# Pairs' weights reach the expert table by indirect word transfers in place of one-hot products

## The chip, the cores and the metric

The kernel runs on one core of one Trainium2 chip. Its time is the device time of one execution in microseconds (us), and lower is better. All times of one core here agree closely: three runs of the kernel before lie between 1845.62 and 1847.0 us. TensorE is called PE in the profile, VectorE DVE, ScalarE ACT, GpSimd POOL (Pool) and SyncE SP.

## What is computed

One decoder block for 512 tokens of 1024 values: an HGRN2 mixer and a dilated-window attention in parallel, then a PEER layer that picks experts. The change lies in the PEER layer alone. For each token and each of 8 heads, 16 of 128 x 128 experts are picked by two lists of 128 keys; expert number = i1 * 128 + i2.

```python
def peer_ffn(x, w_q, sub_keys, u, v):
    q = (x @ w_q).reshape(B, S, PEER_HEADS, 2, PEER_HALF)
    s = jnp.einsum('bshpc,hpnc->bshpn', q, sub_keys).astype(jnp.float32)
    s1, i1 = lax.top_k(s[..., 0, :], PEER_TOPK)
    s2, i2 = lax.top_k(s[..., 1, :], PEER_TOPK)
    ...
    top_s, pos = lax.top_k(cand_s, PEER_TOPK)
    idx = jnp.take_along_axis(cand_i, pos, axis=-1)
    gate = jax.nn.softmax(top_s, axis=-1)
    ...
        hid = jnp.einsum('thkd,td->thk', u[ib], xb)
        a = jax.nn.gelu(hid.astype(jnp.float32), approximate=False) * gb
        return jnp.einsum('thk,thkd->td', a.astype(x.dtype), v[ib])
```

A pair is one token with one picked expert: 512 x 8 x 16 = 65536 pairs. Two heads of one token may pick the same expert, and then their weights add up.

## The kernel before

**Tiles.** The 512 tokens are four tiles of 128, T = 0 to 3. Tiles 1 and 2 (`UD`) take the hidden values u.x of all 16384 experts by streaming the whole of u through PE. Tiles 0 and 3 (`UG`) gather the 128 rows of u that each token's pairs name. Tiles 1, 2 and 0 (`VD`) take the product with v by streaming the whole of v; tile 3 gathers its rows of v. A gather is one indirect transfer from Pool's queue of 128 rows of 4 KB, one for each token, and an instruction of DVE uses it (`u_steps`, L626; `v_steps`, L645; the transfer is issued at L618).

**The table.** The streamed product with v works by blocks b of 128 experts (all i1 for one i2). For that it needs a table of weights [i1, i2, token] that is zero except at the pairs. Before, `scatter_steps` makes it for 16 tokens at a time: DVE compares the pairs' key numbers with a ramp (one-hot rows `e12`, L666), multiplies those of i2 by the weights in three bfloat16 parts (`eg`, L670; for some groups ACT makes the third part, L674), PE multiplies the two for each token (three products a token, L680), ACT copies the result into `Gx` (L682), and SP writes it to DRAM (`g_d`, L685). The first eight blocks of tiles 0 and 2 stay on chip in `Gcs[0]` by a copy of Pool (L687). `thirds` makes the three parts, and `routing` ends with transposes of the key numbers and gates for it.

**Stages.** (1) `Front(0)`: the mixers of the first 256 tokens, with weights loaded by SP and split into two parts; the profile ends it near 300 us. (2) `Front(1)`: the mixers of the second half. Between its loads `background` puts steps of two queues of work: `rows` (gathers of tile 0) and `scat` (the table of tile 1). `routing(0)` and `routing(1)` lie here too; the latter's key numbers are ready at 566 us. (3) The stage between: `routing(2)`, the table of tiles 1, 0 and 2, `NPRE` = 46 calls of `hidden(b)`, and `routing(3)`. `hidden` loads a 512 KB block of u (`ub`), splits it (`uh` on ACT, `ul` on Pool for the first 46, on DVE after), makes 24 matmuls (`ph`) and a Gelu into `pre`, of which there are `RING` = 58 places. (4) The main loop of 128 blocks: the table of eight blocks comes in one load `Gc` (L822); DVE multiplies it by `pre` (L825); it and a 512 KB block of v (`vb`) are split in two; 18 matmuls `acc` follow (L834); then `hidden(b + NPRE)`, and two gather steps of tile 3.

**Order.** The instructions of each engine run in the order that a planner sets when the program is built: it follows the program's order where operands are expected to be ready, and takes later work where they aren't. What waits at the head of an engine's queue holds all behind it. A place of the ring `pre` lets up to 58 hidden blocks stand ahead of the main loop.

Of the kernel before, what the change touches and what calls it, by code (L numbers as in the profile page):

```python
# [8 lines left out]
F32 = mybir.dt.float32  # L9
# [9 lines left out]
P = 128  # L19
S = 512  # L20
D = 1024
# [16 lines left out]
# Token tiles by how the expert layer reaches them: rows of u gathered, u streamed whole, v streamed whole.  # L38
# VD starts with UD; the tile that is not in it gathers its rows of v.
# [5 lines left out]
GT = 16  # L45
NGT = NV // GT
GB = 8
# the first weights' low halves are Pool's
LPOOL = 4
# steps of gathering and scattering before the end of the second half's mixers  # L50
ROWS_P, SCAT_PP = 99, 5
# blocks of hidden values ahead of the products with v, and places for them
NPRE, RING = 46, 58
# tokens in a group of the scatter, groups in flight; groups whose third part ACT scales
GS, EGB = 4, 2
ACT3 = {1: (0, 4, 8, 12), 0: (0, 4, 8, 12), 2: (0, 8)}
ROWS_F, ROWS_D, SCAT_F = 3, 2.0, 0.4
UK, WBUFS, ATB = 4, 4, 3

# columns of the packed per-partition parameters  # L60
C_G1, C_HGN, C_LB, C_QG, C_KG, C_END = 0, 8, 9, 17, 18, 19
# columns of the packed shape constants
M_ATT, M_HG, M_END = 0, 512, 640
# slots of the packed dense weights
# [4 lines left out]
def kernel(ctx: ExitStack, tc: tile.TileContext, x, wst, par, cst, cols, g2, keys, u, v, ut, vr, out):  # L69
# [9 lines left out]
    nc.scalar.activation(root, eps[:, 0:1], AF.Sqrt)  # L79
    h2g = {}  # L80
# [17 lines left out]
    def accumulate(out, ws, xs, cut, w_stays):  # L98
        """Sum over the blocks of w x, in three products where they come in two parts."""
# [24 lines left out]
    # lower bound: softmax over the two logit rows, row 0  # L124
# [5 lines left out]
    # values of the first group by token; of the other two with every fourth token's in a row  # L130
# [13 lines left out]
    class Front:  # L144
        """The mixers of one half of the tokens, and the queries of their expert layer."""

        def __init__(self, h, hi_pool, after_unit):
# [5 lines left out]
            for t in range(NT):  # L153
# [5 lines left out]
                for c in range(0, KC, 4):  # L159
# [20 lines left out]
        def slot(self, i, ks=slice(0, KC)):  # L180
            """Row blocks ks of a slot's weights, UK of them in a tile: the blocks' operands in order."""
# [14 lines left out]
        def proj(self, i, x, T):  # L196
            """A slot's 256 columns of the half's products with x, on the partitions (T) or along them."""
# [112 lines left out]
        def proj_attn(self):  # L310
# [47 lines left out]
            # with the scores' scale of 1 / 8  # L358
# [69 lines left out]
        def proj_gates(self):  # L428
# [6 lines left out]
            # behind the last exponential: the functions' tables take turns  # L435
# [5 lines left out]
        def post(self):  # L441
            """Merge, output projection, second norm and expert queries."""
# [22 lines left out]
            for b in range(4):  # L465
# [13 lines left out]
            for t in range(NT):  # L479
# [21 lines left out]
                # x1 waits in the output rows it belongs to  # L501
# [21 lines left out]
    def thirds(i, x):  # L523
        """x as the exact sum of three bfloat16."""
        w, dst = pk3[:, i], pk[:, i, 2:]
        nc.vector.tensor_copy(dst[:, 0], x)
        nc.vector.tensor_tensor(out=w, in0=x, in1=dst[:, 0], op=ALU.subtract)
        nc.vector.tensor_copy(dst[:, 1], w)
# [374 lines left out]
```

## Time and profile before

| | |
|---|---|
| median of three runs | 1846.65 us (1845.62 to 1847.0) |
| profiled execution: span | 1845.0 us |
| PE busy | 1674.0 us |
| DVE busy | 1444.1 us |
| ACT busy | 795.6 us |
| Pool busy | 793.6 us |
| moved by DMA | 475.61 MB, 258 GB/s over the span |

The profiled execution's own time is its span, 1845.0 us; the median is 1.65 us longer. Busy time is an average over stages, so the stages are read one by one. A PE that is busy isn't PE at its peak: the granted clock (1.00 is 2.4 GHz, 0.50 is 1.2 GHz) has to be read beside it. Pool counts an indirect transfer as busy for the time in which it writes out the transfer's descriptors, not for the time in which the data move.

### The profile page before, as it was taken

Reading aid. Unit: us, or ns where it says so; the run is one execution under the profiler, and the core shown is the slowest. Engines: PE = TensorE matmul, PEld = TensorE weight load, DVE = VectorE, ACT = ScalarE, POOL = GpSimd, SP = SyncE. Lnnn points to the kernel's source line nnn. Section 1 sums busy time; section 2 is a strip of 40 time slices with the busy share of each in tenths; the row PEclk is TensorE's granted clock in tenths of the full one; section 3 lists DMA queues with packets and bytes.
Section 4 is the critical chain, followed back from the end, with each engine's and each line's share of the span. In section 5 each row is a group of like instructions: output and inputs, shape, how many; then the busy total and the mean of one; then the engine's idle time right before and its main releaser. Section 6 shows DMA issues by size and latency. Waiting matters only on the chain.

```text
span 1845.0 us, 28370 instructions
## 1 busy us (share of the span) xinstructions
PE 1674.0 (91%) x10573; PEld 1482.8 (80%) x10573; DVE 1444.1 (78%) x2681; ACT 795.6 (43%) x1348; POOL 793.6 (43%) x546
## 2 busy tenths in 40 slices
PE   6999889889789989888867899999999999999987
PEld 6998888667667878777867878888888888888766
DVE  5644547887887758999999977877877788888777
ACT  5655551211114556368756534343343434343232
POOL 3211312463664335556566543344323464444442
PEclk9999999988899989889978899999999999999999
DMA  6453553778787887534455799999988999999887
GB/s 196 153 158 119 175 194 118 270 235 276 244 279 264 297 298 261 183 111 145 152 183 202 238 372 334 339 328 326 367 298 299 345 339 341 340 340 317 288 309 278
DMA packets 169963, 475.61 MB, mean 258 GB/s; under 512 B 14304, under 2 KB 62688, under 8 KB 168800
## 3 DMA queue, kind: packets, MB, share of 16 engines
q1 hardware_dynamic: 112416, 270.56, 43.0%
q0 software_dynamic: 55296, 201.35, 30.9%
q10 hardware_dynamic: 2112, 1.88, 0.3%
q8 instruction: 83, 1.36, 0.3%
q14 instruction: 56, 0.46, 0.1%
HBM read 443.85 MB, written 28.84 MB: 256 GB/s over the span
## 4 chain that ended last, share of the span: by engine, by line
PE 47%; DVE 25%; DMA 11%; issue 9%; POOL 5%; ACT 1%; DVEq 0%; POOLq 0%; SPq 0%; ACTq 0%
PE acc L834 19%; PE pp L109 13%; PE ph L109 10%; DMA row<-in_u_dram,idx 6%; DVE row L626 4%; DVE e L666 4%; DVE eg L670 3%; POOL row L618 3%; DMA Gc<-g_d 3%; PE pg L680 2%; PE pr L680 1%; DVE cs L564 1%; DVE rest L515 1%; DVE ti L514 1%; DVE h2g L645 1%
## 5 line engine op out<-in xcount | busy, mean ns | idle before, releaser
L618 POOL DMA_INDIRECT row<-in_u_dram,idx x206 | 254.9, 1237 | 383.8 <-DVE row L626 274.3
L626 DVE SCALAR_TENSOR_TENSOR row<-row,h2g 128x1024 f32<-128x1024 f32 x206 | 272.4, 1328 | 62.2 <-DMA row<-in_u_dram,idx 61.3
L109 PE MATMUL ph<-hH,uh 128*128 128x256 f32 x1024 | 302.1, 295 | 7.1 <-ACT pre L792 6.0
L109 PE MATMUL ph<-hH,ul 128*128 128x256 f32 x1024 | 302.9, 296 | 5.0 <-POOL ul L95 5.0
L109 PE MATMUL ph<-hL,uh 128*128 128x256 f32 x1024 | 299.0, 292 | 0.0
L834 PE MATMUL acc<-vl,ah 128*128 128x512 f32 x768 | 241.8, 396 | 9.3 <-DVE vl L95 9.3
L834 PE MATMUL acc<-vh,al 128*128 128x512 f32 x768 | 240.0, 393 | 0.0
L94 ACT ACTIVATE uh<-ub 128x1024 fp32r<-128x1024 f32 x128 | 136.7, 1068 | 230.7 <-PE ph L109 214.1
L834 PE MATMUL acc<-vh,ah 128*128 128x512 f32 x768 | 222.5, 395 | 9.9 <-ACT vh L94 9.9
L109 PEld LDWEIGHTS ph<-hH,uh 128*128 128x128 f32 x1024 | 205.9, 201 | 12.8 <-ACT pre L792 7.8
L109 PEld LDWEIGHTS ph<-hH,ul 128*128 128x128 f32 x1024 | 205.5, 201 | 6.3 <-POOL ul L95 5.8
L109 PEld LDWEIGHTS ph<-hL,uh 128*128 128x128 f32 x1024 | 204.6, 200 | 3.8
L680 PEld LDWEIGHTS <-e 128*128 128x128 bf16 x1152 | 124.8, 119 | 73.4 <-DVE eg L670 65.4
L834 PEld LDWEIGHTS acc<-vl,ah 128*128 128x128 f32 x768 | 143.2, 190 | 40.0 <-DVE vl L95 11.8
L834 PEld LDWEIGHTS acc<-vh,ah 128*128 128x128 f32 x768 | 142.9, 190 | 38.2 <-ACT vh L94 10.5
L834 PEld LDWEIGHTS acc<-vh,al 128*128 128x128 f32 x768 | 145.5, 190 | 31.8
L94 ACT ACTIVATE ah<-Gc 128x384 fp32r<-128x384 f32 x128 | 66.9, 523 | 229.4 <-PE acc L834 226.7
L95 DVE TENSOR_TENSOR vl<-vb,vh 128x1024 fp32r<-128x1024 f32 x128 | 156.1, 1219 | 12.2 <-ACT vh L94 12.0
L618 POOL DMA_INDIRECT row<-in_v_dram,idx x76 | 111.6, 1469 | 120.0 <-DVE h2g L645 109.2
L680 PE MATMUL pg<-eg,e 128*128 128x128 bf16 x768 | 103.1, 297 | 51.8 <-DVE eg L670 51.3
L94 ACT ACTIVATE vh<-vb 128x1024 fp32r<-128x1024 f32 x128 | 135.6, 1059 | 28.6 <-DMA vb<-in_vr_dram 27.9
L674 ACT ACTIVATE eg<-e,pk 128x128 bf16<-128x128 bf16 x320 | 115.4, 565 | 70.9 <-DVE e L666 68.1
(279 smaller groups left out, 3582.4 us busy)
## 6 DMA issues: line engine op xcount, KB each, us to landing
w<-in_wst_dram SPq DMA_DIRECT2D x140, 512.0 KB
ub<-in_ut_dram SPq DMA_DIRECT2D x128, 512.0 KB
vb<-in_vr_dram SPq DMA_DIRECT2D x128, 512.0 KB
Gc<-g_d SPq DMA_DIRECT2D x15, 1536.0 KB
g_d<-Gx SPq DMA_DIRECT2D x16, 960.0 KB
g_d<-Gx SPq DMA_DIRECT2D x8, 1024.0 KB
row<-in_u_dram,idx POOLq DMA_INDIRECT x206
sc<-in_x_dram SPq DMA_DIRECT2D x4, 512.0 KB
```

The source lines that it names most:

```text
L94: nc.scalar.activation(hi, x, AF.Copy)
L95: (eng or nc.vector).tensor_tensor(out=lo, in0=x, in1=hi.bitcast(F32), op=ALU.subtract)
L109: nc.tensor.matmul(out, l, r, start=(i == 0), stop=(i == len(ops) - 1))
L514: nc.vector.max_index(out=ids[:, 0:8], in_max=vals[:, 0:8], in_values=src)
L515: nc.vector.match_replace(out=rest[:, :w], in_to_replace=vals[:, 0:8], in_values=src, imm_value=-BIG)
L618: nc.gpsimd.indirect_dma_start(out=r, out_offset=None, in_=src, in_offset=bass.IndirectOffsetOnAxis(ap=index, axis=0))
L626: nc.vector.scalar_tensor_tensor(r, r, 1.0, h2g[T], op0=ALU.mult, op1=ALU.mult, accum_out=hid[:, g, j:j + 1])
L666: nc.vector.tensor_tensor(out=e12, in0=iota[:, None].to_broadcast([P, 2, NKEY, GS]), in1=e[:, 0:2].to_broadcast([P, 2, NKEY, GS]), op=ALU. ...
L670: last_e2[0] = nc.vector.tensor_tensor(out=eg[:, :n], in0=e12[:, 1:2].to_broadcast([P, n, NKEY, GS]), in1=e[:, 2:2 + n].to_broadcast([P, n ...
L674: nc.scalar.activation(eg[:, 2, :, q], e12[:, 1, :, q], AF.Copy, scale=pk3[:, VD.index(T), i + k + q:i + k + q + 1])
L680: nc.tensor.matmul(pt[:, q], e12[:, 0, :, q0 + q], eg[:, j, :, q0 + q], start=(j == 0), stop=(j == 2))
L834: nc.tensor.matmul(acc[t][c], lt, r[:, c * 512:(c + 1) * 512], start=(b == 0 and i == 0), stop=(b == NKEY - 1 and i == 2))
```

## The change

The table [i1, i2, token] of each tile in `VD` lies in DRAM by itself. It is cleared during `Front(0)` by twelve transfers of 2 MB from ACT's queue, one behind every fourth load of weights. `routing` only makes, for each pair, its place in the table (128 x expert number + token) in one instruction of DVE. `spread_steps` then issues, for each of a tile's 128 pairs of a token (8 heads x 16), one indirect transfer of 128 words, one a token, that adds the word to the table. The 16 transfers of a head wait for all 16 of the head before, so that no two additions to one word are under way at once; the loads of `Gc` wait for the last head of each tile. For tiles 1 and 2 the words are the gates, and for tile 0 they are the gates times the Gelu of the gathered hidden values.

One-hot rows, their products, ACT's copies, `thirds` and the transposes in `routing` are gone. `Gc` is loaded in three transfers of 512 KB, in runs of 4 KB, where it was one of 1536 KB in runs of 512 B. `ul` of all hidden blocks is DVE's. `NPRE` goes from 46 to 60 and `RING` from 58 to 72. `routing(3)` and the gathers of tile 3 come between the hidden blocks, from b = 16 on, half a gather for each block; in the main loop it is 1.9 for each. Removed comments are left out below.

```diff
-GT = 16
-NGT = NV // GT
+ROWS_P, SCAT_PP = 99, 110
+NPRE, RING = 60, 72
+ROWS_F, ROWS_H, ROWS_D, SCAT_F = 3, 0.5, 1.9, 3
+RT3 = 16
...
+    tok = const.tile([P, 1], F32, name="tok")
+    nc.scalar.dma_start(out=tok, in_=par[:, C_TOK:C_TOK + 1])
...
         if T in VD:
-            pt = route_bank(T)
-            i12 = rt.tile([P, 2, P], F32, name="i12")
...
-            if T in UD:
-                nc.tensor.transpose(pt[:, 3], gate, ident)
-                thirds(VD.index(T), pt[:, 3])
+            nc.vector.tensor_scalar(place[:, VD.index(T)], full, float(P), tok, op0=ALU.mult, op1=ALU.add)
...
-    def scatter_steps(T, bank):
...
+    def spread_steps(T):
+        i = VD.index(T)
+        w = gates[:, T] if T in UD else hid[:, UG.index(T)]
+        for j in range(P):
+            d = nc.gpsimd.indirect_dma_start(out=g_d[i].rearrange("i j t -> (i j t)")[:, None], in_=w[:, j:j + 1],
+                                             out_offset=bass.IndirectOffsetOnAxis(ap=place[:, i, j:j + 1], axis=0),
+                                             in_offset=None, compute_op=ALU.add)
...
+            if j % TOPK == 0:
+                before, spread[i] = spread[i], []
+            behind(d, before)
+            spread[i].append(d)
             yield 1
...
+        zero = whi.tile([P, D], F32, name="zero", bufs=1)
+        nc.gpsimd.memset(zero, 0.0)
+        clear = [(g, k) for g in g_d for k in range(0, NKEY, 32)]
+        def clearing(load):
+            if f_units[0] % 4 == 3 and clear:
+                g, k = clear.pop(0)
+                with tc.issue_after(load.ins):
+                    nc.scalar.dma_start(out=g[:, k:k + 32].rearrange("p (a b) t -> p a (b t)", b=8),
+                                        in_=zero[:, None].to_broadcast([P, 4, D]))
...
-    scat.add(scatter_steps(1, pr_bank))
+    scat.add(spread_steps(1))
...
+    scat.add(spread_steps(0))
...
-        ubs = halves(us.tile([P, KC, P], F32R, name="uh"), us.tile([P, KC, P], F32R, name="ul"), ub,
-                     nc.gpsimd if b < NPRE else nc.vector)
+        ubs = halves(us.tile([P, KC, P], F32R, name="uh"), us.tile([P, KC, P], F32R, name="ul"), ub)
...
         routing(2, rq2)
-        scat.add(scatter_steps(0, pg_bank))
-        scat.add(scatter_steps(2, pg_bank))
-        scat(P)
+        scat.add(spread_steps(2))
+        scat(2 * P)
         for b in range(NPRE):
+            if b == RT3:
+                routing(3, rq3)
+                h2g[3] = const.tile([P, D], F32, name="h2g")
+                nc.sync.dma_start(out=h2g[3], in_=h2_d)
+                rows.add(u_steps(3))
             hidden(b, php)
-        routing(3, rq3)
...
+            rows(ROWS_H)
...
         if b % GB == 0:
-            Gc = Gcs[0]
-            if b:
-                Gc = (vs if b // GB % 2 else dp).tile([P, NGT, GB, GT], F32, name="Gc", bufs=1)
-                nc.sync.dma_start(out=Gc, in_=g_d[:, :, b:b + GB])
+            Gc = (vs if b // GB % 2 else dp).tile([P, len(VD), GB, P], F32, name="Gc", bufs=1)
+            for t, g in enumerate(g_d):
+                behind(nc.sync.dma_start(out=Gc[:, t], in_=g[:, b:b + GB]), spread[t])
```

## Rows read from the trace of the kernel before

**Rows 1.** Stages; columns: length, busy us (instructions) by engine, granted clock, DMA share, GB/s.

```profile
565.00:1066.00 501.00, 417.81 (x2912) 384.80 (x2910) 439.92 (x907) 303.88 (x589) 268.76 (x174) 0.90 0.63 214
1066.00:1845.00 779.00, 752.51 (x4128) 653.57 (x4128) 622.68 (x795) 289.92 (x407) 320.33 (x228) 0.98 0.92 327
```

**Rows 2.** Chain that ended last, main loop; columns: start us, length us, what.

```profile
1126.00 2.84 PE ph L109 x24
1128.84 4.14 PE acc L834 x18
...
1453.94 17.67 DMA Gc<-g_d
...
1710.00 16.46 DMA Gc<-g_d
...
1754.29 19.05 DMA Gc<-g_d
...
1778.99 54.50 PE acc L834 x237
```

**Rows 3.** Groups by line, the scatter's; columns: busy us, mean ns, idle before, releasers.

```profile
L674 ACT ACTIVATE eg<-e,pk 128x128 bf16<-128x128 bf16 x320 | 115.4, 565 | 70.9 <-DVE e L666 68.1 <-DVE pk L529 2.7
L666 DVE TENSOR_TENSOR e<-iota,pk 128x1024 bf16<-128x1024 bf16 x96 | 103.8, 1089 | 27.5 <-PE pr L680 20.7 <-PE pg L680 6.6
L680 PE MATMUL pg<-eg,e 128*128 128x128 bf16 x768 | 103.1, 297 | 51.8 <-DVE eg L670 51.3 <-issue 0.3
L670 DVE TENSOR_TENSOR eg<-e,pk 128x1024 bf16<-128x1024 bf16 x96 | 103.0, 1082 | 0.1
...
L680 PE MATMUL pr<-eg,e 128*128 128x128 bf16 x384 | 50.0, 297 | 6.4 <-DVE eg L670 4.2 <-ACT eg L674 2.0
```

**Rows 4.** Instructions on tile e: duration ns min/median/max, first and last start us.

```profile
L666 DVE TENSOR_TENSOR e<-iota,pk x96: 660/686/3107, 567.5 to 1044.1; 128x1024 bf16<-128x1024 bf16 x96
```

**Rows 5.** Pool in order of time; columns: start us, length us, instruction, idle before it.

```profile
918.30 1.35 POOL L618 DMA_INDIRECT row<-in_u_dram,idx  x1 [0.30 <-issue]
919.96 0.94 POOL L618 DMA_INDIRECT row<-in_u_dram,idx  x1 [0.30 <-issue]
921.20 1.05 POOL L618 DMA_INDIRECT rq<-in_u_dram,idx  x1 [0.30 <-issue]
922.55 0.94 POOL L618 DMA_INDIRECT rq<-in_u_dram,idx  x1 [0.30 <-issue]
923.51 2.35 POOL L95 TENSOR_TENSOR ul<-ub,uh 128x1024 fp32r<-128x1024 f32 x1
```

**Rows 6.** Stages, gathers (line 618) alone; columns: length, Pool busy us (count), clock, DMA.

```profile
0.00:565.00 565.00, 95.28 (x81) 0.94 0.62 202
565.00:1066.00 501.00, 88.66 (x76) 0.90 0.63 214
```

**Rows 7.** Groups by line: Pool's part of routing, and the split of u on DVE.

```profile
L95 DVE TENSOR_TENSOR ul<-ub,uh 128x1024 fp32r<-128x1024 f32 x82 | 101.1, 1233 | 53.7 <-ACT uh L94 51.6 <-ACT ah L94 1.2 <-issue 0.7
...
L582 POOL TENSOR_TENSOR sel<-eq,ci 128x800 f32<-128x800 bf16 x32 | 54.5, 1704 | 56.1 <-DVE eq L580 55.9
...
L584 POOL TENSOR_TENSOR sel<-sel 128x400 f32<-128x400 f32 x32 | 40.8, 1276 | 0.7
```

**Rows 8.** Chain that ended last, second half's mixers: gathers from issue to use.

```profile
316.67 10.17 DMA row<-in_u_dram,idx
...
555.09 5.29 DMA row<-in_u_dram,idx
```

**Rows 9.** Stages, tile ph alone; columns: length, busy PE, PEld, ACT, clock, DMA.

```profile
565.00:1066.00 501.00, 192.20 (x1248) 177.94 (x1248) 18.94 (x51) 0.90 0.63 214
```

**Rows 10.** DMA queues of the page: packets, MB, share of 16 engines' span.

```profile
q0 software_dynamic: 55296, 201.35, 30.9%
q10 hardware_dynamic: 2112, 1.88, 0.3%
```

More of the change, by code (lines that the diff above doesn't have):

```diff
@@ L44 @@
 NV = len(VD) * P
-GT = 16
-NGT = NV // GT
 GB = 8
+GS = 4
 LPOOL = 4
[L51 to L57, printed above, removed]
+ROWS_P, SCAT_PP = 99, 110
+NPRE, RING = 60, 72
+ROWS_F, ROWS_H, ROWS_D, SCAT_F = 3, 0.5, 1.9, 3
+RT3 = 16
 UK, WBUFS, ATB = 4, 4, 3
-C_G1, C_HGN, C_LB, C_QG, C_KG, C_END = 0, 8, 9, 17, 18, 19
+C_G1, C_HGN, C_LB, C_QG, C_KG, C_TOK, C_END = 0, 8, 9, 17, 18, 19, 20
 M_ATT, M_HG, M_END = 0, 512, 640
@@ L521, in route_bank @@
         return pt.rearrange("p (n k) -> p n k", k=NKEY)
[L523 to L528, printed above, removed]
-        nc.vector.tensor_tensor(out=w, in0=w, in1=dst[:, 1], op=ALU.subtract)
-        nc.vector.tensor_copy(dst[:, 2], w)
     def routing(T, rq):
         gate = gates[:, T]
-        full = rt.tile([P, P], F32, name="full")
+        full = fulls[:, VD.index(T)] if T in VD else rt.tile([P, P], F32, name="full")
         sv = rt.tile([P, PH, TOPK], F32, name="sv")
@@ new lines, with behind @@
+    spread = {i: [] for i in range(len(VD))}
+    def behind(d, others):
+        for o in others:
+            tc.add_manual_dep(d.ins, o.ins.name, mybir.DependencyInfo(mybir.DependencyClass.Sync, mybir.DependencyReason.DATA),
+                              reason="pairs of one expert")
+    def spread_steps(T):
[5 more added lines that the diff above has]
+                                             in_offset=None, compute_op=ALU.add)
+            tc.declare_no_dep(d.ins, group=f"spread{i}{j // TOPK}", reason="heads are ordered below")
+            tc.add_to_no_dep_group(f"spread{i}{j // TOPK}", d.ins)
+            if j % TOPK == 0:
+                before, spread[i] = spread[i], []
+            behind(d, before)
+            spread[i].append(d)
@@ L711 @@
     rows, scat = Pump(), Pump()
+    dram = ctx.enter_context(tc.tile_pool(name="dram", bufs=1, space=bass.MemoryType.DRAM))
+    h2_d = dram.tile([P, D], F32, name="h2_d")
+    g_d = [dram.tile([P, NKEY, P], F32, name=f"g_d{i}") for i in range(len(VD))]
     rq_pool = ctx.enter_context(tc.tile_pool(name="rq", bufs=2, side="left"))
@@ L742 @@
     hid = gat.tile([P, len(UG), P], F32, name="hid", bufs=1)
-    pk = gat.tile([P, len(VD), 5, P], BF16, name="pk", bufs=1)
-    pk3 = gat.tile([P, len(VD), P], F32, name="pk3", bufs=1)
     rctx = ctx.enter_context(ExitStack())
-    gb = rctx.enter_context(tc.tile_pool(name="gb", bufs=1, side="left", **TILE))
     rt = rctx.enter_context(tc.tile_pool(name="rt", bufs=1, side="left", **TILE))
+    fulls = rt.tile([P, len(VD), P], F32, name="fulls", bufs=1)
+    place = rt.tile([P, len(VD), P], I32, name="place", bufs=1)
     pr = rctx.enter_context(tc.tile_pool(name="pr", bufs=2, space=PSUM, side="left"))
@@ L760 @@
     routing(1, rq1)
-    pr_bank = lambda: pr.tile([P, 512], F32, name="pr")
-    scat.add(scatter_steps(1, pr_bank))
+    scat.add(spread_steps(1))
     f.hgrn(0)
@@ L778 @@
     pre = []
-    Gcs = [dp.tile([P, NGT, GB, GT], F32, name="Gc")]
-    nc.sync.dma_start(out=Gcs[0][:, :P // GT], in_=g_d[:, :P // GT, :GB])
     def hidden(b, pool):
@@ L792, in hidden @@
         nc.scalar.activation(dst, pt, AF.Gelu)
-    with tc.tile_pool(name="php", bufs=2, space=PSUM, side="right") as php, \
-            tc.tile_pool(name="pg", bufs=3, space=PSUM, side="right") as pg:
-        pg_bank = lambda: pg.tile([P, 512], F32, name="pg")
+    with tc.tile_pool(name="php", bufs=4, space=PSUM, side="right") as php:
         routing(2, rq2)
-        scat.add(scatter_steps(0, pg_bank))
-        scat.add(scatter_steps(2, pg_bank))
-        scat(P)
+        scat.add(spread_steps(2))
+        scat(2 * P)
         for b in range(NPRE):
-            hidden(b, php)
-        routing(3, rq3)
-    h2g[3] = const.tile([P, D], F32, name="h2g")
-    nc.sync.dma_start(out=h2g[3], in_=h2_d)
-    rows.add(u_steps(3))
-    with tc.issue_after(last_e2[0].ins):
-        rows(4)
+            if b == RT3:
[3 more added lines that the diff above has]
+                rows.add(u_steps(3))
+            hidden(b, php)
+            rows(ROWS_H)
     rows.add(v_steps(3))
@@ L831 @@
             for i, (l, r) in enumerate([(aH, vH), (aH, vL), (aL, vH)]):
-                lt = l.rearrange("p g t -> p (g t)")[:, t * P:(t + 1) * P]
+                lt = l[:, t]
                 for c in range(2):
```

55 lines of the change are left out of this document (7 added, 48 removed).

## The prediction, made before the changed kernel was seen

> **What bounds the kernel now.** I read the stages first, then the chain of work that ended last, then the groups by line for what the change touches, and last the order of time on Pool, because the change moves its work there.
>
> The stages split at two points. Up to 565 us the mixers run, and the change hardly touches them. From 565 to 1066 us the table is made. Here DVE is busy for 440 of 501 us, Pool for 269, and PE for 418 at a clock of 0.90; from 1066 on PE is busy for 753 of 779 us at 0.98 [rows 1]. So the stage between is DVE's, and the main loop is PE's.
>
> What ends the stage between is the table: the one-hot instructions of DVE run from 567.5 to 1044.1 us [rows 4], and the products with v can't start before all three tiles are in it. The main loop adds up from the chain: a hidden block costs PE 2.84 us and a block of v 4.14 [rows 2]. 1248 of the `ph` matmuls, 52 blocks of 24, lie before 1066 [rows 9], so PE still owes 76 x 2.84 + 128 x 4.14 = 216 + 530 = 746 us. From the end of the last matmuls (1778.99 + 54.50 = 1833.5 [rows 2]) to the span's end there are 11.5 us. 1066 + 746 + 11.5 = 1823.5; the 21 us that are missing to 1845 fit the three late loads of `Gc`, which stand in the chain with 16 to 19 us each, partly behind earlier PE work [rows 2].
>
> So the end is M + what PE owes at M, where M is the start of the products with v. Both terms change.
>
> **What goes.** DVE loses 103.8 + 103.0 us of one-hot work, ACT 115.4 and its copies of the products, PE 1152 matmuls with 153 us of busy time [rows 3]. On DVE and PE this is time of the stage between, and none of it is in the main loop [rows 4]. DVE gets `ul` of the first blocks from Pool: 60 x 1.233 = 74 us [rows 7]. DVE then needs 440 - 207 - 7 (the three-part split and the transposed numbers, an estimate from its few short instructions) + 74 = 300 us in that stage; at its former share of 440 / 501 it would be through at 565 + 300 / 0.88 = 906. If nothing else bound it, M would be there. The gain on DVE is real, but it isn't the end of the sum.
>
> **What comes.** Pool gets 384 indirect transfers of words. The trace shows none of them; the nearest row is the gather of 128 rows, which also has 128 places, one for each token. Where Pool has nothing to wait for, a gather takes 0.94 us and the next starts 0.30 us later: 919.96 to 921.20 is 1.24 us [rows 5]. Bounds of the cadence: below, 0.94 with hardly any gap (Pool's next instruction of another kind follows in 0.02 us [rows 5]), 0.96; above, the stage's mean of 88.66 / 76 = 1.17 [rows 6] and the gap, 1.47. A word is less than a row for the DMA engines, but Pool writes the descriptor of a place, not its bytes; the addition may need more of it, and the missing wait for a buffer less. I take 1.24, the row nearest in kind and undisturbed.
>
> The words of tile 1 can start when `routing(1)` is through, at 565 as before. From there to M Pool must do: the 128 - 81 = 47 gathers of tile 0 that are left [rows 6] and 384 words, 431 x 1.24 = 534 us; its part of `routing(2)` and `routing(3)`, half of 54.5 + 40.8, 48 us [rows 7]; four additions of the mixers, about 7 us; and of the up to 22 gathers of tile 3 that stand between the hidden blocks, half, 14 us. Together 603.
>
> **The heads.** A tile's next head waits at the head of Pool's queue, and behind it stand the other tiles' words, the gathers and the routing steps that DVE waits for. A gather takes 5.3 to 10.2 us from issue to use [rows 8], with 512 KB in it. With 8 heads a tile, 7 of them waiting, 21 such waits are 111 to 214 us if nothing lies between, and nothing if two tiles take turns. Tile 1 is alone with the gathers at first, tiles 0 and 2 can alternate: I take four bare waits of 5.3, 21 us.
>
> By the Trainium skill, "DMA: Bandwidth & Descriptors", section "Anatomy of one DMA — SWDGE (gpsimd) path", a transfer that Pool issues has a fixed cost of about 2.0 us, most of it the receipt of the last write, and the heaviest target is DRAM. By that the 21 waits would be 42 us at most, and the four 8. No row here shows a bare transfer of words, so it stays at the gather's 5.3.
>
> **Smaller parts.** The clearing is 24 MB during the first mixers, whose stage up to 565 has a DMA share of 0.62 at 202 GB/s [rows 6]. It is hidden under PE while the loads of weights keep their lead; without that cover it costs 24 MB at the main loop's 327 GB/s [rows 1], 73 us. I take 4. PE's relief at the end of the second mixers is worth nothing while Pool is behind. After the last head there is its landing (5), the first `Gc` (8, as three small gathers) and its product and split (7, from the first step after the stall at 1453.94 to the matmuls): 20 us.
>
> M = 565 + 4 + 603 + 21 + 20 = 1213, where it was 1066.
>
> **What PE owes at M.** Before, 52 blocks were done between `NPRE` 46 and `RING` 58; I take the middle of 60 and 72 again, 66. 62 x 2.84 + 530 = 706. The loads of `Gc` in runs of 4 KB should be late less often: 10 us of the 21. With the 11.5 at the end: 728.
>
> 1213 + 728 = 1941, against the profiled span of 1845.0; the median lies 1.65 above that span. **Forecast: 1940 us, slower by 5%.** The one-hot work leaves DVE and PE, which were full, but the table gets done on Pool, which was half idle, and in a queue of one after another that needs longer than DVE did.
>
> **Rivals.**
>
> *A word is cheap on Pool (faster).* Place: Pool's queue from 565 to M. If the 0.30 us before a gather belongs to its wait for a buffer, or a word's descriptor to less work, the cadence falls. At 0.96 the sum loses 384 x 0.28 = 107 us: 1833. At half a gather, 0.62, it loses 238: 1702. It decides against my sign from 1.24 - 97 / 384 = 0.99 us on. For it: Pool follows a transfer by another instruction in 0.02 us. Against it: four gathers in a row all show 0.30 [rows 5]. I give it 1780 and 0.27.
>
> *The words bind the DMA engines (much slower).* Place: the same stage, on 16 engines. 384 word transfers have as many packets as the 384 gathers that make up q0, 55296. A gather's packet takes 0.309 x 16 x 1845 us / 55296 = 165 ns, a packet of q10 with 890 bytes 0.003 x 16 x 1845 / 2112 = 42 ns [rows 10]. The stage used 0.63 x 501 = 316 us of every engine [rows 1]. With 3456 packets an engine, the words fit into the 648 us up to M while one takes under 96 ns. An addition in DRAM reads and writes; at 165 ns it needs 570 us, M becomes 565 + 316 + 570 + 20 = 1471, and the end 2199. Waits for heads lengthen in the same case, since a head's last word lands behind its queue. I give it 2150 and 0.15.
>
> The Trainium skill, "DMA: Bandwidth & Descriptors", section "Specifications", speaks for this one: under 512 B a DMA engine reads, modifies and writes. By that rule every word is two passes over memory. No row here has such a packet.
>
> *It comes out even.* Where the cadence is near 0.99 the two sides meet: 0.04, 1846.
>
> **How the numbers follow.** The forecast, slower by 1% to 8%, has 0.54; the cheap word 0.27; the full DMA engines 0.15; even 0.04. Some 0.2% is what a measurement of this kernel can tell from no change. Faster is 0.27, same 0.04, slower 0.69. The forecast's own range takes the cadence from 1.05 to 1.47 and the heads from none to half of 214: 1860 to 2070. The range for 8 in 10 takes in part of the first rival, down to a cadence of about 0.9 (1800), and part of the second, up to some 125 ns a word packet (565 + 316 + 432 + 20 + 728 = 2061, and a little for the heads): 1800 to 2080.
>
> **What would show it.** Right: Pool nearly without a gap from 565 to the first `acc` matmul, words 1.2 to 1.3 us apart, the chain through Pool's queue there, PE idle with its ring of 72 full, first `acc` near 1210, and then 6.98 us for each block with a hidden block in it. The first rival: words under 1 us apart, first `acc` before 1110, and the chain on DVE or PE. The second: Pool waiting at every 16th word, or short instructions with long gaps; a DMA share near 1 with few GB/s. The forecast is wrong above all if words cost Pool less than rows do, and it errs on the high side if the planner puts words ahead of what else Pool has to do.

## The result, and the profile after

After the change the kernel takes 2245.12 us (median of four, 2238.74 to 2248.49), before it 1846.83 in the same runs: a ratio of 1.2147, 95% interval 1.2115 to 1.218. It is slower by 21%. The direction and the place of the loss are those of the forecast, the size isn't: 305 us over 1940, outside the range. The profiled execution took 2246.77 us, 1.87 more than its span of 2244.9.

The first 300 us of the kernel after, and its two later stages, cut where its words start (585) and at the first product with v (1554); columns as in [rows 1]: length, busy us (instructions) of PE, PEld, DVE, ACT and Pool, granted clock, DMA share, GB/s.

```profile
0.00:300.00 300.00, 234.72 (x1999) 221.97 (x2000) 120.78 (x196) 133.10 (x213) 61.14 (x32) 0.97 0.61 219
...
585.00:1554.00 969.00, 388.84 (x2520) 354.81 (x2520) 336.91 (x823) 143.29 (x234) 802.83 (x514) 0.70 0.50 114
1554.00:2245.00 691.00, 672.54 (x3504) 576.80 (x3504) 583.38 (x751) 256.29 (x354) 298.19 (x220) 0.99 0.92 342
```

The stage between takes 969 us where it took 501 [rows 1], and in it Pool is the only engine that is busy for most of the time. DVE, which had 440 of 501 us, has 337 of 969, and PE 389. The main loop is shorter: 691 us, not 779.

The words on Pool, by tile of the table: duration in ns (min/median/max), first and last start.

```profile
L643 POOL DMA_INDIRECT g_d<-gates,place x256: 1547/1552/2692, 584.9 to 1517.1; - x128
L643 POOL DMA_INDIRECT g_d<-hid,place x128: 1551/1556/2654, 1075.6 to 1471.7; - x128
```

Three of them in order of time (start, length, what, idle time before it):

```profile
1300.00 1.55 POOL L643 DMA_INDIRECT g_d<-hid,place  x1 [0.30 <-issue]
1301.85 1.55 POOL L643 DMA_INDIRECT g_d<-hid,place  x1 [0.30 <-issue]
1303.71 1.55 POOL L643 DMA_INDIRECT g_d<-hid,place  x1 [0.30 <-issue]
```

Line 643 alone, from 585 to 1519: length, Pool busy us (count), clock, DMA share, GB/s.

```profile
585.00:1519.00 934.00, 639.76 (x384) 0.70 0.49 107
```

An adding word transfer takes Pool 1.55 us, and the next starts 0.30 us later: 1.855 us where nothing disturbs, against 1.24 of a gather [rows 5]. Over the stage it is more: 639.76 us busy for 384, and 115.4 us of idle time before them (76.6 + 38.8, below), 1.97 us a word.

The groups by line, of PE's wait and of the words: busy us, mean ns, idle time before, and what ended most of it.

```profile
L110 PE MATMUL ph<-hH,uh 128*128 128x256 f32 x1024 | 304.0, 297 | 370.0 <-ACT pre L770 338.7
L643 POOL DMA_INDIRECT g_d<-gates,place x256 | 425.3, 1661 | 78.7 <-issue 76.6
L643 POOL DMA_INDIRECT g_d<-hid,place x128 | 214.5, 1676 | 38.8 <-issue 38.8
```

A stretch late in the words, in the columns of the first fence:

```profile
1200.00:1520.00 320.00, 7.91 (x61) 7.30 (x60) 29.32 (x51) 3.71 (x5) 269.27 (x177) 0.52 0.30 33
```

PE waits 338.7 us for `pre`, 314 of them in one wait that ends at 1524.8: the ring of 72 places is full, and no product with v can take a block out. From 1200 to 1520 us hardly any engine but Pool works. The DMA engines are 0.30 busy there and move 33 GB/s, so they aren't the bound. "issue" as the releaser means that the profile shows nothing for which a word waited.

The Trainium skill describes this picture in "Perfetto Trace Analysis", section "What 'DMA-bound' means": a kernel can be bound by the queue that issues transfers, whose track is then solid with slices that are the writing of descriptors, not the moving of data. The rows agree as far as they go: the words hold Pool for 755 of the 934 us from 585 to 1519, gaps included, at a DMA share of 0.49.

The chain of waits at the end of the stage (start, length, what):

```profile
1517.08 1.55 POOL g_d L643
1518.63 1.07 POOL sel L576
...
1522.98 5.84 DMA row<-in_u_dram,idx
...
1541.49 1.14 DVE ul L96
1542.84 0.15 SPq L766
1543.09 0.38 SPq L800
...
1545.42 17.44 DMA Gc<-g_d
```

SP's issues there, in order of time:

```profile
1520.18 0.33 SPq L795 DMA_DIRECT2D Gc<-g_d  x1
1536.50 6.49 SPq L766 DMA_DIRECT2D ub<-in_ut_dram  x2
1543.09 1.54 SPq L800 DMA_DIRECT2D vb<-in_vr_dram  x3
```

The last word ends at 1518.6, the first product starts at 1553.8. In these 35 us SP issues `Gc`, which waited for the last word at the head of its queue, then two blocks of u, and only then the first blocks of v. Most of the time goes to the blocks of u: 22.6 us lie between the issues of `Gc` (1520.5) and of v (1543.1), and for 21.8 of them SP waits for DVE ahead of the two blocks: 15.9 us end with a `ul`, 5.9 just behind the next `ul`. This instruction is the last to read a block of u, and here it stands on DVE among the gather steps of tile 3.

The start is late too. ACT from 13 to 53 us, in order of time (start, length, what, idle before it):

```profile
13.89 15.93 ACTq L693 DMA_DIRECT2D g_d<-zero  x3
29.86 1.06 ACT L95 ACTIVATE wh<-w 128x1024 fp32r<-128x1024 f32 x1 [15.70 <-issue]
29.88 5.30 ACTq L693 DMA_DIRECT2D g_d<-zero  x1
35.23 0.63 ACT L95 ACTIVATE hH<-pT 128x512 fp32r<-128x512 f32 x1 [4.31 <-issue]
35.25 16.72 ACTq L693 DMA_DIRECT2D g_d<-zero  x3
52.02 0.63 ACT L95 ACTIVATE hH<-pT 128x512 fp32r<-128x512 f32 x1 [16.17 <-issue]
```

All twelve clearing transfers are issued between 4.4 and 52.1 us, not one behind every fourth load: the order was set against loads on SP's queue, and ACT's queue didn't wait for these (SP had issued at most eight loads of weights by then). While ACT issues them, it does nothing else for 4 to 16 us at a time. PE gets its first `hH` late and is busy for 235 of the first 300 us. In the kernel before it was 273:

```profile
0.00:300.00 300.00, 273.48 (x2331) 258.55 (x2332) 158.97 (x287) 153.41 (x252) 63.89 (x32) 0.98 0.50 157
```

### The profile page after: what moved, and what is told of

It is laid out like the page before. It is cut to its first block, busy times and chain, and to the rows that moved or that the text cites. A ratio compares the mean times of both kernels' runs of the same rounds, so it can differ in the third digit from the quotient of the medians.

```text
span 2244.9 us, 25786 instructions
## 1 busy us (share of the span) xinstructions
PE 1543.9 (69%) x9412; PEld 1363.0 (61%) x9412; DVE 1274.6 (57%) x2511; ACT 597.4 (27%) x932; POOL 1292.4 (58%) x869
## 3 DMA queue, kind: packets, MB, share of 16 engines
q0 software_dynamic: 110592, 201.57, 32.4%
## 4 chain that ended last, share of the span: by engine, by line
PE 25%; POOL 20%; issue 6%; DMA 3%; DVE 1%; ACT 0%; SPq 0%; DVEq 0%; POOLq 0%; ACTq 0%
PE acc L806 18%; POOL g_d L643 17%; PE ph L110 6%; POOL row L599 1%; DMA vb<-in_vr_dram 1%; POOL rq L599 1%; DMA Gc<-g_d 1%; DMA rq<-in_v_dram,idx 0%; DMA g_d<-gates,place 0%; DMA row<-in_u_dram,idx 0%; POOL sel L576 0%; DVE row L607 0%; DVE idf L577 0%; ACT vh L95 0%; DVE h2g L622 0%
## 5 line engine op out<-in xcount | busy, mean ns | idle before, releaser
L110 PE MATMUL ph<-hH,uh 128*128 128x256 f32 x1024 | 304.0, 297 | 370.0 <-ACT pre L770 338.7
L643 POOL DMA_INDIRECT g_d<-gates,place x256 | 425.3, 1661 | 78.7 <-issue 76.6
L607 DVE SCALAR_TENSOR_TENSOR row<-row,h2g 128x1024 f32<-128x1024 f32 x206 | 277.3, 1349 | 223.9 <-DMA row<-in_u_dram,idx 223.3
L599 POOL DMA_INDIRECT row<-in_u_dram,idx x206 | 249.2, 1210 | 252.0 <-DVE row L607 147.6
L643 POOL DMA_INDIRECT g_d<-hid,place x128 | 214.5, 1676 | 38.8 <-issue 38.8
L806 PE MATMUL acc<-vh,ah 128*128 128x512 f32 x768 | 208.8, 392 | 10.0 <-ACT vh L95 10.0
L96 DVE TENSOR_TENSOR ul<-ub,uh 128x1024 fp32r<-128x1024 f32 x128 | 160.3, 1253 | 89.5 <-ACT uh L95 87.9
L577 DVE TENSOR_REDUCE idf<-sel 128x16 f32<-128x400 f32 x32 | 26.3, 823 | 314.6 <-POOL sel L576 314.6
L96 POOL TENSOR_TENSOR wl<-w,wh 128x1024 fp32r<-128x1024 f32 (+1 forms) x22 | 55.2, 2511 | 251.0 <-ACT wh L95 197.2
L599 POOL DMA_INDIRECT row<-in_v_dram,idx x76 | 105.8, 1392 | 109.1 <-DVE h2g L622 101.5
```

Source lines behind the costliest of these rows:

```text
L96: (eng or nc.vector).tensor_tensor(out=lo, in0=x, in1=hi.bitcast(F32), op=ALU.subtract)
L110: nc.tensor.matmul(out, l, r, start=(i == 0), stop=(i == len(ops) - 1))
L577: nc.vector.tensor_reduce(out=idf[:, n], in_=sel[:, :hc].rearrange("p c k -> p k c"), axis=AX.X, op=ALU.add)
L599: nc.gpsimd.indirect_dma_start(out=r, out_offset=None, in_=src, in_offset=bass.IndirectOffsetOnAxis(ap=index, axis=0))
L607: nc.vector.scalar_tensor_tensor(r, r, 1.0, h2g[T], op0=ALU.mult, op1=ALU.mult, accum_out=hid[:, g, j:j + 1])
L643: d = nc.gpsimd.indirect_dma_start(out=g_d[i].rearrange("i j t -> (i j t)")[:, None], in_=w[:, j:j + 1], out_offset=bass.IndirectOffsetOnA ...
```

## The experiments

Each run was timed in three rounds beside the kernel before; the ratio is to it. The theory is that Pool's time for a word is the mis-sized term. Rivals are the waits between heads, the DMA engines, the clearing, and the work of tile 3.

### Half of the words, and a quarter

```diff
-        for j in range(P):
+        for j in range(P // 2):
```

In the second run it is `P // 4`.

> Only the first 64 of each tile's 128 words a token are sent, so half of the pairs are missing. In the changed kernel the 384 word transfers stand on Pool 1.97 us apart (1.67 us busy and a gap of 0.30) from 585 to 1519 us, and Pool has hardly another gap there. If that issue alone sets the start of the products with v (theory 1), 192 transfers fewer bring it forward by 192 x 1.97 = 377 us and the time to about 1870 us. If the wait for each head sets it (theory 2), half of the heads goes too, but the words' own cadence is then not what is left and the gain should be nearer to 100 us, about 2140. If it is the clearing or the moved split of u (theory 3), the time stays near 2245.

> Leaves out 96 of the 128 words of each tile (six of eight heads), so 96 word transfers in all; the weights of the other pairs are missing from the table. Theory 1 (Pool's queue of words sets the start of the products with v): from 64 to 32 words a tile the last word comes 96 x 1.97 = 189 us sooner than with half of the words, first product with v near 1030 where it was 1217. But in the run with half of the words only some 50 hidden blocks were done by 1030, so PE owes 77 x 2.84 + 530 + 22 = 771 us there, not 695: about 1800 us. If Pool's queue were still all of it, the time would fall by as much per word as from 384 to 192 words (1.71 us): 1753 us. Under the theory that PE and DVE already bind with half of the words: no gain, 1900 us.

Half: 1916.97 us, ratio 1.0383 (1.0356 to 1.0411). Quarter: 1790.14 us, ratio 0.9686 (0.9643 to 0.973). The words of the run with half, as in the fence on the words, and its products with v:

```profile
L643 POOL DMA_INDIRECT g_d<-gates,place x128: 1552/1556/2617, 585.2 to 1168.0; - x128
...
L806 PE MATMUL acc<-vh,ah x768: 387/389/501, 1217.1 to 1889.8; 128*128 128x512 f32 x192
```

The same of the run with a quarter:

```profile
L643 POOL DMA_INDIRECT g_d<-gates,place x64: 1551/1556/2582, 587.6 to 982.4; - x64
...
L806 PE MATMUL acc<-vh,ah x768: 387/389/500, 1056.9 to 1774.1; 128*128 128x512 f32 x192
```

192 words fewer end 349 us sooner (1517.1 to 1168.0), 1.82 us a word, and the kernel is 328 us faster; the 1870 expected was 47 too low. With 96 words the first product comes at 1057 where 1030 was expected, PE has 734 us left and not 771, and the time is near the 1800 of the theory. It is faster than the kernel before, but three quarters of the weights are missing from its table. Here the next limits show. Between the starts of the last word and of the first product lie 75 us, with 13 blocks of u ahead of v on SP's queue; in the run with half it is 49 us with five blocks, and in the kernel after 37 with two. And the words, gaps included, hold Pool for only 208 of the 396 us in which they are sent; gathers that wait for DVE stand between them. Even so, from half to a quarter the last word comes 1.93 us sooner for each word left out, and M 1.67 us, so M still hangs on the words there.

### Write the word, or fetch it, in place of adding it

```diff
-                                             in_offset=None, compute_op=ALU.add)
+                                             in_offset=None)
```

> The words are written, not added, so where two heads name one expert only the later word is left. If the addition is why a word takes Pool 1.55 us where a gather of rows takes 0.94, each word falls to about 0.95 and the cadence from 1.97 to 1.36: 384 x 0.61 = 234 us less, 2010. If it is the word or the direction (from the core to DRAM), the words stay at 1.55 and the time at 2245.

2019.03 us, ratio 1.0924 (1.0887 to 1.0961). Its words:

```profile
L643 POOL DMA_INDIRECT g_d<-gates,place x256: 965/970/2052, 582.8 to 1290.9; - x128
```

In the second run the same 384 transfers fetch a word from the table into an unused tile:

```diff
-            d = nc.gpsimd.indirect_dma_start(out=g_d[i].rearrange("i j t -> (i j t)")[:, None], in_=w[:, j:j + 1],
-                                             out_offset=bass.IndirectOffsetOnAxis(ap=place[:, i, j:j + 1], axis=0),
-                                             in_offset=None, compute_op=ALU.add)
+            d = nc.gpsimd.indirect_dma_start(out=back[:, i, j:j + 1], out_offset=None, in_=g_d[i].rearrange("i j t -> (i j t)")[:, None],
+                                             in_offset=bass.IndirectOffsetOnAxis(ap=place[:, i, j:j + 1], axis=0))
```

> The same 384 transfers run the other way: each fetches a word for each token from its place in the cleared table into a scratch tile, so the table stays zero. If a word costs Pool what a row costs, and the addition is the rest, a transfer takes 0.94 us and the time is near 2010. If short transfers cost Pool more whatever their direction, it takes 1.55 and the time stays near 2245.

1973.31 us, ratio 1.0684 (1.0658 to 1.071). Its words:

```profile
L643 POOL DMA_INDIRECT back<-g_d,place x384: 940/945/1979, 463.7 to 1223.0; - x192
```

A fetched word takes 0.945 us, as long as the fetched row of 4 KB before (0.94 [rows 5]): here the size didn't matter to Pool. A written one takes 0.970, an added one 1.552. That is 0.58 us for the addition, 384 x 0.58 = 223 us, and the time fell by 226. This is the main part of the miss. The fetches start at 464 since tile 0's needn't wait for its weights, so that run's time isn't the price of a fetch alone.

### Half of the places in each transfer

```diff
-            d = nc.gpsimd.indirect_dma_start(out=g_d[i].rearrange("i j t -> (i j t)")[:, None], in_=w[:, j:j + 1],
-                                             out_offset=bass.IndirectOffsetOnAxis(ap=place[:, i, j:j + 1], axis=0),
+            d = nc.gpsimd.indirect_dma_start(out=g_d[i].rearrange("i j t -> (i j t)")[:, None], in_=w[:64, j:j + 1],
+                                             out_offset=bass.IndirectOffsetOnAxis(ap=place[:64, i, j:j + 1], axis=0),
```

The second run has this edit and leaves out the addition too, as above.

> All 384 adding word transfers, each with the words of tokens 0 to 63 of the tile only; the weights of the other 64 tokens are missing from the table. Theory 1 (Pool's time for a word transfer is by the place, one descriptor each, and the addition makes each descriptor dearer): 64 places cost about half of 1.55, so 0.8 to 1.0 us, a cadence of 1.1 to 1.3, first product with v near 1240 to 1320 and a time of 1930 to 2020 us. Rival (the addition costs a fixed time for each instruction, not for each place): the time of a write, 0.97, may halve, but the 0.58 of the addition stays: 1.07 to 1.3 us. Second rival (all of it is fixed): 1.55 us, 2245 us.

> 384 word transfers that write and don't add, each with the words of tokens 0 to 63 of its tile; the sums of double picks and the weights of the other 64 tokens are missing from the table. From 64 to 128 places an adding transfer took 1.41 and 1.55 us, so 0.0022 us a place and 1.27 that no place costs; a writing one of 128 places took 0.97. Theory (the addition is a fixed extra time of an instruction, some 0.58 us): 64 places written take 0.97 - 0.14 = 0.83 us, cadence 1.13, and about 384 x 0.14 = 54 us less than with 128 places: 1965 us. Rival (a writing transfer's time is by the place): 0.5 us, 1830 to 1860 us.

Adding: 2187.08 us, ratio 1.1836 (1.1784 to 1.1889). Its words:

```profile
L643 POOL DMA_INDIRECT g_d<-gates,place x256: 1398/1410/2511, 588.9 to 1466.6; - x128
```

Writing: 1991.46 us, ratio 1.078 (1.0733 to 1.0826). Its words:

```profile
L643 POOL DMA_INDIRECT g_d<-gates,place x256: 892/897/1980, 584.6 to 1263.1; - x128
```

My theory of a price by the place falls: half the places save 0.142 us of 1.552 when adding and 0.073 of 0.970 when writing. If the time is a fixed part and a part by the place, a place costs 2.2 or 1.1 ns, and what no place costs is 1.27 or 0.82 us. Less than a fifth of a word transfer's time on Pool is for its words. A fixed price of the addition misses as well, by less: 0.83 us and 1965 were expected of 64 written places, and the addition takes 0.51 us more with 64 places and 0.58 with 128. The four durations and times fall on one line: 384 x (1.552 - 0.897) = 252 us, and 2245 - 1991 = 254. The Trainium skill, "DMA: Bandwidth & Descriptors", section "Anatomy of one DMA — SWDGE (gpsimd) path", says that one can emit a lot of descriptors before their incremental cost shows. The 1 to 2 ns a place agree. It puts the fixed cost of some 2.0 us chiefly into the completion; here the part that bound is Pool's 0.82 to 1.27 us and the 0.30 behind it, which every transfer pays in turn.

### No waits between heads

A table for each head, with the waits left out; the weights of seven heads go to tables that nothing reads.

```diff
-            d = nc.gpsimd.indirect_dma_start(out=g_d[i].rearrange("i j t -> (i j t)")[:, None], in_=w[:, j:j + 1],
+            d = nc.gpsimd.indirect_dma_start(out=g_h[i][j // TOPK].rearrange("i j t -> (i j t)")[:, None], in_=w[:, j:j + 1],
...
-                before, spread[i] = spread[i], []
-            behind(d, before)
+                spread[i] = []
```

> Each head's words go to a table of its own, so no transfer waits for another head; only the first head's tables are cleared and read, so the sums over heads are left out. The number of words, their kind and the wait of the loads of the table for the last words stay. Theory 1 (Pool's issue): 21 waits cost 20 us at most, 2225 to 2245. Theory 2 (the heads' waits, 21 of 5.3 to 10 us): 2035 to 2135.

2260.45 us, ratio 1.2235 (1.2207 to 1.2263). Without the waits the kernel isn't faster but 15 us slower, above the range expected. In the kernel after, Pool's idle time for a head is 1.8 us ahead of words and 2.8 ahead of gathers; in this run the profile puts 1.5 us down to the same, though no word waits for a head. In this run a word lands 3.0 us after its issue (median), and in the kernel after there was nearly always another tile's word or a gather to issue meanwhile. So the waits cost next to nothing; the trace of the kernel after says so better than this run's time, since the planner's order changed as well. The last word starts at 1490.2 here, 27 us sooner, with 57 gathers ahead of it and not 77. The first product comes 76 us behind it, at 1566.5, and SP's issues before it (with `vb` next, at 1559.08) are eight blocks of u:

```profile
1509.61 45.29 SPq L766 DMA_DIRECT2D ub<-in_ut_dram  x8
```

### The clearing on SP's queue

```diff
-                    nc.scalar.dma_start(out=g[:, k:k + 32].rearrange("p (a b) t -> p a (b t)", b=8),
+                    nc.sync.dma_start(out=g[:, k:k + 32].rearrange("p (a b) t -> p a (b t)", b=8),
```

> The twelve clearing transfers go out on SP's queue, where each stands behind the load that it follows, not on ACT's queue, where all twelve went out between 4 and 52 us. Theory 1 (the late start of the words, 584.9 us where the one-hot work started at 567.5, is ACT being held while it issues the clearing): PE no longer waits for ACT's hH at the start, the words start near 567, and the whole end moves by the same 16 to 19 us: about 2227 us. Rival (the start is late because 24 MB are moved at all, beside the weights): the loads of weights come later instead, words from 580 or later, 2240 to 2260 us.

2198.02 us, ratio 1.1887 (1.1829 to 1.1945). Its start, in the columns of the first fence of all:

```profile
0.00:300.00 300.00, 272.73 (x2298) 258.43 (x2299) 149.61 (x249) 150.41 (x249) 62.61 (x33) 0.97 0.68 238
```

Its words:

```profile
L643 POOL DMA_INDIRECT g_d<-gates,place x256: 1547/1558/2633, 544.3 to 1473.1; - x128
```

The words start 41 us sooner, and the end comes 47 us sooner, where I expected 16 to 19. I had measured the delay against the one-hot work's start at 567.5 [rows 4]. With the clearing out of ACT's way they start at 544, ahead of that, so the clearing also hid a gain of 23 us. Where this gain comes from no run tells. It isn't the one-hot work itself, since the kernel before has none ahead of 567.5. The 24 MB themselves cost nothing that shows: PE is busy for 273 of the first 300 us, with all of it moved.

### Tile 3's work behind the hidden blocks

```diff
-ROWS_F, ROWS_H, ROWS_D, SCAT_F = 3, 0.5, 1.9, 3
+ROWS_F, ROWS_H, ROWS_D, SCAT_F = 3, 0, 2.0, 3
-RT3 = 16
+RT3 = 59
```

> routing(3) goes behind the hidden blocks of the stage between (before block 59 of 60, not 16), no gathers of tile 3 stand between these blocks, and the main loop takes 2.0 gathers a block as before. Theory 1 (the 35 us from the last word to the first product with v, and some 20 gathers and half of a routing step on Pool, come from tile 3's work in that stage): the last word comes some 40 to 50 us sooner, the first product with v follows in about 20, near 1490, and the time is 2180 to 2200 us. Rival (tile 3's work stands ahead of the products with v in any case, or the main loop pays for it): first product after 1530, or a main loop that is longer by what it is sooner: 2235 to 2260 us.

2244.06 us, ratio 1.2158 (1.2102 to 1.2213). The last word starts at 1515.0, not 1517.1, and of `sel` as many steps (15 and 14, where there were 14 and 14) lie before it. The planner put the work where it was, so this run tells that the order in the program isn't the order on the engines; what tile 3's work costs there stays open.

### Both terms taken back together

Words written, not added, and the clearing on SP's queue: the two edits above in one kernel.

> The words written and not added (so that the sums of double picks are missing), and the clearing on SP's queue. The two mis-sized terms of the prediction taken back together: if they add up, 2019 - 47 = 1972 us, and against the forecast's 1940 only 384 x 0.03 us of cadence (1.27, not 1.24) and some 20 us of contention and of the way from the last word to the first product stay. Rival (the two overlap, since with cheaper words Pool is not always the late one): 1990 us or more.

1968.97 us, ratio 1.0675 (1.064 to 1.0711). The two add up (1972 expected). With a word near the price that I had put into the sum, and the clearing hidden as I had assumed, the time is 29 us above the forecast.

### Only one tile by words

The kernel before, with one tile's table reached by 128 words and the other two by one-hot products, its `ul` shared between Pool and DVE, four clearing transfers on SP's queue. Tile 1 by words in the first three, tile 2 in the last two.

```diff
-    scat.add(scatter_steps(1, pr_bank))
+    scat.add(spread_steps())
...
-                     nc.gpsimd if b < NPRE else nc.vector)
+                     nc.gpsimd if b < NPRE and b % 2 else nc.vector)
```

> The kernel before, with the table of tile 1 alone reached by words (128 transfers into a table of its own, four clearing transfers on SP's queue); tiles 0 and 2 keep their one-hot products. ul of every second early hidden block moves from Pool to DVE. Theory 1 (a word costs Pool 1.97 us, which is cheap only where Pool has that time to spare): DVE loses a third of its one-hot work, 69 us, and gets 23 x 1.23 = 28 us; Pool gets 128 x 1.97 = 252 us and loses 23 x 2.35 = 54. Before, Pool was busy for 269 of the 501 us of the stage, so 467 now; DVE 400. The stage ends near 1030 to 1060 where it ended at 1066: 1805 to 1840 us. Rival (Pool is the bound even so, since gathers of tile 0, which the one-hot work of tile 0 waits for, queue behind words): 1850 to 1900 us.

> As h_a, but ul of hidden blocks 0 to 19 is DVE's and of 20 to 45 Pool's, so that no ul queues behind the words, which come first. Theory 1: 1805 to 1840 us, at or below h_a. If where ul stands does not matter: as h_a within 5 us.

> As h_a, but a third as many words (1, not 3) are put behind each load of the second mixers, so that the gathers of tile 0 come ahead of them. Theory 1: the one-hot work of tile 0 starts sooner: 1800 to 1840 us, up to 15 us below h_a. If the order in the program does not set the order on Pool: as h_a within 5 us.

Tile 1: 1978.07 us, ratio 1.07 (1.066 to 1.0741); 1965.62, 1.0616 (1.0573 to 1.0659); 1983.25, 1.0726 (1.0686 to 1.0766). All missed theory 1 by over 100 us. These runs also shift `ul`, so they price the arrangement and not the words alone. DVE's one-hot work in the first, and its products with v (by tile, as the words):

```profile
L698 DVE TENSOR_TENSOR eg<-e,pk x64: 661/686/2060, 950.8 to 1200.2; 128x1024 bf16<-128x1024 bf16 x48, 128x1536 bf16<-128x1536 bf16 x16
...
L878 PE MATMUL acc<-vh,ah x768: 387/390/794, 1218.6 to 1964.9; 128*128 128x512 f32 x192
```

The one-hot work of tile 0 needs that tile's hidden values, and its gathers stand between the words on Pool: `hid` is ready at 946 us, where it was 773 in the kernel before, and DVE makes all of `eg` after that. With words at a third of the rate behind each load (the third run) the order didn't change enough to help.

> The kernel before with tile 2, not tile 1, reached by words: they come behind the gathers of tile 0 and routing(2), three for each hidden block, and one-hot products of tiles 1 and 0 run beside them. ul of every second early hidden block is DVE's, four clearing transfers on SP's queue. Theory 1 (a word's price matters only where Pool is late, and in the runs with tile 1 by words it was late for the gathers of tile 0, whose one-hot work started at 950 us): the one-hot work runs from 545 on, and the first product with v comes at 1030 to 1070: 1810 to 1850 us. Rival (the words of tile 2, which can start only when routing(2) is through, now end last): first product 1100 to 1150, 1870 to 1920 us.

> As h2_a, but routing(2) comes ahead of the rest of tile 1's one-hot work in the program and six words stand ahead of each hidden block, so that the words of tile 2 start sooner. Theory 1: 1800 to 1840 us, below h2_a if there the words end last. Rival (the order on the engines stays the planner's): as h2_a within 10 us.

Tile 2: 1960.68 us, ratio 1.0616 (1.0581 to 1.0651), and 1950.89, ratio 1.0568 (1.0535 to 1.0601). The words of the last:

```profile
L677 POOL DMA_INDIRECT g_d<-gates,place x128: 1543/1544/2595, 859.4 to 1174.8; - x128
```

Now the one-hot work runs from 570 to 918, as it should, but `place` of tile 2 is ready only at 859, and 128 words with Pool's other work need 316 us from there. Both miss theory 1 by 111 us, and the second is within the 10 us of the first that its rival gave. So words for one tile lose as well, by what they hold up or by what they come behind. None of the kernels that compute everything beats the kernel before.

## Why the prediction was wrong, step by step

The sum was M + what PE owes: 1213 + 728 = 1941. The trace has 1553.8 + 691 = 2245. So M is out by 341 us and PE's part by -37.

**The price of a word is the step that failed.** Predicted 1.24 us, the gather's cadence; in the stage it was 1.966 (755.2 / 384). 384 x 0.726 = 279 us of the 341. Of that, 384 x 0.615 = 236 is the undisturbed word (1.855), most of it the addition's 0.58, and the remaining 43 the mean over the median (1.66 and 1.55). Line 643 alone, in the columns of its fence above:

```profile
585.00:1200.00 615.00, 395.80 (x231) 0.79 0.59 146
1200.00:1519.00 319.00, 243.96 (x154) 0.52 0.30 33
```

So some 37 of these 43 us lie before 1200 us, where the other engines are busy too (1.71 us a word, and 1.58 from there on). Why some words take up to 2.7 us no run tells. My argument, that Pool writes the descriptor of a place and not its bytes, was right on the bytes and wrong on what followed. The upper bound of 1.47 came from gathers as well, so that the sentence "the addition may need more of it" had no number of its own in the range. At the two upper ends that it names, 1.47 us a word and 107 us of heads in place of 21, the sum gives 1941 + 384 x 0.23 + 86 = 2115, so the 2070 and 2080 were written too low; 2115 doesn't hold the time either. Bounded by a second pass, 2 x 0.94 + 0.30 = 2.18, the sum would have gone up to 1941 + 384 x 0.94 = 2302, and a range up to there would have held the time.

**The start.** 585, not 569: 16 us. I let the clearing cost 4 us under PE's cover, and left out the queue that it is issued from and what ACT has behind it. That step was also wrong on the other side: once the clearing is out of the way the words start 23 us sooner than 567.5, a gain that no term of the sum has. It isn't the relief of PE that I called worth nothing, since no product of the table lay ahead of 567.5 before.

**Gathers.** 77 stood between the words, not 58, because fewer were done by the late start (71, not 81) and more of tile 3's came in; with their waits they took some 123 us of Pool, not 72: 51 us. It is the rest of the 934 us from 585 to 1519, after 755 of words, 49 of `sel`, 5 of additions and 2 of heads.

**Heads.** 21 us predicted, some 2 measured ahead of words (the 2.8 ahead of gathers are counted there). The planner let tiles and gathers take turns, and the run without the waits was no faster.

**From the last word to the first product.** 35 us, not 20. I counted the landing and DVE's steps, and missed SP's queue: the blocks of v stand behind the waiting `Gc`, and then behind two blocks of u whose buffers DVE frees late. The runs with more blocks of u in that place (49 us with five, 76 with eight, 75 with 13) fit this; no run changes it alone. These parts are 279 + 16 + 51 - 19 + 15 = 342, against 341.

**What PE owes.** 691, not 728. With a full ring 78 blocks were done by then (1872 / 24 matmuls before the first product and 1200 / 24 = 50 blocks after it), where I took 66. 50 x 2.84 + 530 + 11.5 = 683.5; the 7.5 that are left are late loads, which I had put at 10. The main loop's model holds.

```profile
585.00:1554.00 969.00, 263.39 (x1872) 251.87 (x1872) 28.27 (x77) 0.70 0.50 114
1554.00:2245.00 691.00, 156.27 (x1200) 153.49 (x1200) 18.53 (x51) 0.99 0.92 342
```

(Tile `ph` alone: length, busy PE, PEld and ACT, clock, DMA share, GB/s.)

**The rivals.** The cheap word fell at once. The full DMA engines gave 2150, nearer to the time than my forecast, by a mechanism that isn't there: q0 took 0.324 x 16 x 2244.9 - 0.309 x 16 x 1845 = 2516 us more for 55296 more packets [rows 10], 45 ns each if a gather's packets cost what they did, and 96 was the point from which it would have decided. The rule of the Trainium skill on writes under 512 B ("DMA: Bandwidth & Descriptors", section "Specifications") may hold, but at this price it doesn't bind.

## What to carry to other kernels

An indirect transfer from Pool is priced by the instruction: 0.9 to 1.6 us and 0.30 behind it, whether it moves 64 words or 128 rows of 4 KB. It pays where one instruction carries much, and 128 words are not much: a tile's 128 transfers, 64 KB of weights, cost Pool 250 us here. And an operation with an extra (an addition on the way) is another kind of instruction than the one whose row is at hand; its upper bound needs a price of its own. Here twice that row would have held it.

When work goes to another queue, count what stands behind it there, and also what the issue itself holds: the words started 41 us later for twelve transfers that ACT only had to issue. The same holds for SP's queue, where blocks of u stood ahead of the first v.

## What the runs showed of the hardware

An adding transfer is cut up otherwise than a writing one. Pool's queue in the kernel after has 110592 packets; 384 gathers are 55296 of them [rows 10], so an adding word transfer has 55296 / 384 = 144. Pool's queue in the kernel after (packets, MB, share of 16 engines' span):

```profile
q0 software_dynamic: 110592, 201.57, 32.4%
```

In the run that writes 128 places:

```profile
q0 software_dynamic: 67584, 201.57, 28.6%
```

In the run that adds 64:

```profile
q0 software_dynamic: 86016, 201.47, 30.6%
```

In the run that writes 64:

```profile
q0 software_dynamic: 67584, 201.47, 28.8%
```

The writing one has (67584 - 55296) / 384 = 32, with 128 places and with 64, and the adding one with 64 places 80. So an addition makes a packet for each place, 128 or 64, and 16 more; the packets of a write don't go by its places. That goes with the dearer place (2.2 and 1.1 ns), not with the 0.45 us that the addition costs beside its places. Where Pool spends these is not shown by any run.

ACT's issue of a transfer of 2 MB took 0.4 to 10.2 us (median 4.8) when twelve were issued in a row; on SP, behind loads, the same took 0.4 to 0.6 us.
